# Gate products between the branches' steps, kept in DRAM and read back by the merge: one step of a hybrid decoder on one Trainium2 core

## The chip, the core and the metric

The program runs on one NeuronCore of a Trainium2 chip. The engines are PE (TensorE; PEld is its weight load), DVE (VectorE), ACT (ScalarE), POOL (GpSimd) and SP, whose queue issues most of the DMAs; each executes its own instructions in a fixed order. The metric is the device time of one execution in microseconds (us), the median of several runs. One execution was also taken with the hardware profiler.

## The reference

One layer is computed for a prompt of 1024 tokens and for 8 samples of 8 tokens, with d_model 1024:

```python
n = rmsnorm(x, g_mix);  z = n @ w_in            # gq gk gv gr glr | fq fk fv ff | mq | gt
gates = sigmoid(gt + b_gate).reshape(B, T, 3, 1024)        # gt: 3 * 1024 columns of w_in
o_gla = gla_chunked(...)      # gated linear attention, 4 heads of 128, a state carried over the chunks
o_fox = fox_attend(...)       # softmax attention with forget gates, 8 heads of 64, paged cache for the samples
o_mem = mem_attend(...)       # 4 heads over 256 memory tokens
m = (gates[:, :, 0] * (og @ w_gla_o) + gates[:, :, 1] * (o_fox @ w_fox_o) + gates[:, :, 2] * (o_mem @ w_mem_o))
h = x + m @ w_out
h = h + peer_ffn(rmsnorm(h, g_ffn), ...)   # 8 heads choose 16 of 16384 experts for each token
y = rmsnorm(h, g_final)
```

The expert layer reads one row of two tables (4 KB each) for every token, head and choice. The gates' columns of z depend on the normed input alone; nothing of the branches enters them.

## The kernel before, in words

**Tiling and stages.** The tokens are nine blocks: 0 to 7 of the prompt (128 tokens each) and block 8 with the 64 sample tokens (`SAMPLE`). `base(grp)` computes everything up to the experts' scores for a group of blocks; the groups are [0, 1, 2], [3, 4, 5] and [8, 6, 7], called group 0, 1 and 2 here. NT is the group's number of tokens: 384, 384 and 320. In `base` come: norm and transposes; for each half of the heads the projections, the GLA of each block (`branch1`, then `gla`), the FoX attention (`fox_prompt`); `fox_sample` in group 2; the memory attention; then the merge, the product with w_out, and the scores (w_pq and keys). The part up to the memory attention is called the branch stage below.

**A product.** `mm_w` (L256) loads weights in pieces of 512 KB into one of four `wr` buffers, splits each in two steps into a high part `wh` (ACT, L265) and a low part `wl` (DVE, L267), and multiplies high by high, high by low and low by high. For `proj_T` (L687), which gives a transposed result for 256 columns of w_in, that is 8 x 3 x 2 = 48 matmuls of NT columns (L273, L274, L277), two weight loads, four `wh` and four `wl`. Its results lie in the PSUM banks `pj` (two) and, in group 0, `cw`.

**The merge** (L821 to L842). For each of 3 branches and 4 pieces of 256 columns: one `proj_T` for the gate, the branch's output product (24 matmuls into banks `f`), two sigmoids on ACT from PSUM (L837), and the products and sums on DVE (L839 to L842). So a merge has 12 gate products, 576 matmuls, and 288 matmuls of output products.

**Experts.** Blocks 0, 1, 2, 6 and 7 gather their rows (`peer_gather`): for each, 128 indirect DMAs of 512 KB for u (issued by POOL, L1040; used by DVE, L1042) and 128 for v (L1051; L1057), through four row buffers. Blocks 3, 4, 5 and 8 go through a dense stage at the end (`peer_dense`): both tables are read as a whole, split and multiplied on PE. The weights of that stage (`expert_weights`) are made during group 2. The gathers of blocks 0 to 2 start when group 0 has its scores and run beside groups 1 and 2; those of blocks 6 and 7 start when group 2 has its scores and run beside the dense stage.

**What sets the order.** A scheduler goes through the program by priorities: the code of `base` in the order in which it is written, the choice of experts ahead of it, the gathers far behind. An instruction stands on its engine where the scheduler expects its inputs and a free buffer. The buffers of one name are given out in the order of the program, so a gate product of the merge can only get a `pj` bank when all the projections written before it have had theirs. On the chip each engine then keeps that fixed order.

Of the kernel before, what the change touches and what calls it, by code (L numbers as in the profile page):

```python
# [54 lines left out]
def tile_hybrid(ctx: ExitStack, tc: tile.TileContext, x_prompt, x_sample, cache_fox_k, cache_fox_v,  # L55
# [572 lines left out]
    x2_scr = [dp.tile([128, 1024], F32, name=f"x2_scr{b}") for b in range(9)]  # L628
    o_scr = [dp.tile([128, 3, 4, 128], F32, name=f"o_scr{b}") for b in range(9)]
# [6 lines left out]
    def base(grp):  # L636
# [50 lines left out]
        def proj_T(col):  # L687
            pz, jobs = jobs_T(NT, acT)
            mm_w(wi, 8, col, jobs)
            return pz  # L690

        for half in range(2):
# [45 lines left out]
            branch1(grp[0])  # L738
            kT = T("kv", [128, 2, 1024])
# [37 lines left out]
            for b in grp[1:2]:  # L777
                branch1(b)
            proj(C_FV + half * 256, fin_v)
            for b in grp[2:]:  # L780
                branch1(b)
            pq = proj_T(C_FQ + half * 256)
# [5 lines left out]
            for b in grp:  # L788
                if b != SAMPLE:
                    o = out_tile(b)  # L790
                    fox_prompt(b, half, qT[:, :, off[b]:off[b] + 128], kT, vv, o)
                    put(b, 1, half, o)

        if SAMPLE in grp:
            o = [out_tile(SAMPLE), out_tile(SAMPLE)]
            fox_sample(lfs[0], o)
            for half in range(2):
                put(SAMPLE, 1, half, o[half])
# [21 lines left out]

        m = [T("z", [128, 2, NT]) for _ in range(4)]  # L821
        for br, wo in enumerate((w_gla_o, w_fox_o, w_mem_o)):
# [7 lines left out]
            for c in range(4):  # L830
                pz = proj_T(C_GT + br * 1024 + c * 256)
                po, jobs = jobs_T(NT, (oh, ol), "f")
                mm_w(wo[0], 4, c * 256, jobs)
                for j in range(2):
                    s = T("X", [128, NT])
                    g = br * 8 + c * 2 + j
                    A.activation(s, pz[j], AF.Sigmoid, bias=bgT[:, g:g + 1])  # L837
                    if br == 0:
                        V.tensor_tensor(m[c][:, j], po[j], s, op=OP.mult)  # L839
                    else:  # L840
                        V.tensor_tensor(s, po[j], s, op=OP.mult)
                        V.tensor_tensor(m[c][:, j], m[c][:, j], s, op=OP.add)  # L842
# [397 lines left out]
    def fox_sample(lfn, oT):  # L1240
# [45 lines left out]
        for st in range(4):  # L1286
            pc = [PS("f"), PS("f")]
# [207 lines left out]
```

## Time and profile before

| | |
|---|---|
| device time, median of 3 | 4426.75 us (4417.42 to 4428.59) |
| the profiled execution | 4433.77 us, its span 4432.0 us |
| busy share of the span | PE 85%, PEld 74%, DVE 75%, ACT 41%, POOL 38% |
| HBM traffic | 257 GB/s over the span, 1073 MB read and 64 MB written |
| mean granted TensorE clock | 0.89 |

Busy shares are means over stages that differ; the prediction reads them stage by stage. Matmuls are pipelined: the mean duration of one in the groups is longer than the distance from one to the next, so that the cost of a row of matmuls is read from a stretch of time and the number in it. A wait is put down to the event that came last. Where an engine is idle and is not the one that others wait for, nothing is lost.

### The profile page before, as it was taken

To read this page: it belongs to the slowest core of one execution; us is meant where nothing else is said; L and a number is where in the kernel's file an instruction comes from. 1 tells how busy PE (TensorE), PEld (TensorE's weight loads), DVE (VectorE), ACT (ScalarE), POOL (GpSimd) and SP (SyncE) were. 2 spreads that over 40 slices of the span, in tenths; PEclk is the share of its full clock that TensorE was granted. 3 is DMA by queue.
4 is the path that set the end of the run, shared out by engine and by line. 5 is a ranking of instruction groups with operands and counts; after the bars stand their busy time and mean duration, and the time that the engine had idled before them with its cause. 6 is when DMAs were issued, how large, how long until landed. Compare 5 with 4: busy or idle time off the path is not lost. (4 is left out here: it accounts for less than half of the span.)

```text
span 4432.0 us, 62344 instructions
## 1 busy us (share of the span) xinstructions
PE 3755.6 (85%) x21306; PEld 3288.8 (74%) x21306; DVE 3346.1 (75%) x7924; ACT 1796.2 (41%) x3637; POOL 1679.1 (38%) x1466
## 2 busy tenths in 40 slices
PE   4998998676689775787679979986999999999998
PEld 4886997564378775575556558875999899999997
DVE  3443469988788898888885457578999888888883
ACT  2555444343343333465564334444333223323332
POOL 0000003545644444534455553003445454545530
PEclk8997998787689886677689989997999999999999
DMA  3322457888899987778788899548999999999982
GB/s 110 90 84 70 131 165 227 279 274 294 277 309 332 319 267 242 260 243 273 253 277 287 307 321 320 169 140 289 329 303 339 327 332 337 341 337 327 344 297 81
DMA packets 652340, 1141.32 MB, mean 258 GB/s; under 512 B 62158, under 2 KB 445798, under 8 KB 648439
## 3 DMA queue, kind: packets, MB, share of 16 engines
q0 software_dynamic: 193616, 704.99, 45.6%
q1 hardware_dynamic: 458406, 432.35, 30.3%
q8 instruction: 169, 2.77, 0.2%
q14 instruction: 149, 1.21, 0.1%
HBM read 1073.45 MB, written 63.74 MB: 257 GB/s over the span
## 5 line engine op out<-in xcount | busy, mean ns | idle before, releaser
L1040 POOL DMA_INDIRECT u<-in_peer_u_dram,ei x640 | 783.3, 1224 | 873.2 <-DVE a L1042 347.6
L1051 POOL DMA_INDIRECT v<-in_peer_v_dram,ei x640 | 762.3, 1191 | 865.0 <-DVE acc L1057 452.6
L1042 DVE CUSTOM_DVE_ANT_0 u<-u,x 128x1024 f32<-128x1024 f32 x640 | 774.2, 1219 | 129.9 <-DMA u<-in_peer_u_dram,ei 128.3
L1057 DVE SCALAR_TENSOR_TENSOR acc<-v,a,acc 128x1024 f32<-128x1024 f32 x635 | 811.6, 1278 | 70.6 <-DMA v<-in_peer_v_dram,ei 68.2
L265 ACT ACTIVATE wh<-wr 128x512 fp32r<-128x512 f32 x568 | 354.0, 630 | 595.0 <-PE pj L274 186.2
L267 DVE TENSOR_TENSOR wl<-wr,wh 128x512 fp32r<-128x512 f32 x568 | 386.6, 685 | 219.4 <-PE pj L277 63.8
L1210 PE MATMUL py<-dwh,dvh 128*128 128x448 f32 x1024 | 373.9, 370 | 31.3 <-ACT dwh L1197 28.6
L1187 PE MATMUL pa<-xh,duh 128*128 128x448 f32 x1024 | 384.8, 376 | 1.3 <-ACT duh L1168 1.3
L1188 PE MATMUL pa<-xl,duh 128*128 128x448 f32 x1024 | 379.0, 370 | 0.0
L273 PE MATMUL pj<-aT,wh 128*128 128x384 f32 (+1 forms) x1104 | 367.3, 337 | 11.4 <-ACT X L837 4.5
L1211 PE MATMUL py<-dwl,dvh 128*128 128x448 f32 x1024 | 375.4, 367 | 1.4 <-DVE dwl L1198 1.4
L1212 PE MATMUL py<-dwh,dvl 128*128 128x448 f32 x1024 | 373.4, 368 | 0.3 <-DVE dvl L1206 0.3
L274 PE MATMUL pj<-aT,wh 128*128 128x384 f32 (+1 forms) x1104 | 362.3, 332 | 1.7 <-DVE aT L317 1.7
L281 PE MATMUL pj<-wh,aT 128*128 128x256 f32 x944 | 262.1, 301 | 30.3 <-DVE z L720 10.9
L1205 ACT ACTIVATE dvh<-dvr 128x1024 fp32r<-128x1024 f32 x128 | 134.2, 1059 | 377.2 <-PE py L1211 206.6
L282 PE MATMUL pj<-wh,aT 128*128 128x256 f32 x944 | 258.8, 297 | 2.9 <-DVE aT L847 1.5
L277 PE MATMUL pj<-aT,wl 128*128 128x384 f32 (+1 forms) x1104 | 251.8, 335 | 10.3 <-DVE wl L267 10.1
L1117 PE MATMUL cw<-hot,hot 128*128 128x128 f32 x768 | 173.9, 363 | 92.7 <-ACT stg L1118 73.8
L1190 PE MATMUL pa<-xh,dul 128*128 128x448 f32 x1024 | 240.2, 369 | 0.0
L1117 PEld LDWEIGHTS cw<-hot,hot 128*128 128x128 f32 x768 | 134.8, 248 | 138.1 <-ACT stg L1118 103.3
L1210 PEld LDWEIGHTS py<-dwh,dvh 128*128 128x128 f32 x1024 | 192.4, 189 | 48.6 <-ACT dwh L1197 28.9
L273 PEld LDWEIGHTS pj<-aT,wh 128*128 128x128 f32 x1104 | 213.1, 193 | 17.4 <-ACT X L837 6.6
(475 smaller groups left out, 8439.3 us busy)
## 6 DMA issues: line engine op xcount, KB each, us to landing
wr<-in_w_in_dram SPq DMA_DIRECT2D x168, 512.0 KB, 4.8
dvr<-in_peer_v_dram SPq DMA_DIRECT2D x128, 512.0 KB, 7.5
dur<-in_peer_u_dram SPq DMA_DIRECT2D x128, 512.0 KB, 6.6
dc<-c_scr SPq DMA_DIRECT2D x15, 1792.0 KB, 17.4
wr<-in_w_pq_dram SPq DMA_DIRECT2D x48, 512.0 KB, 4.3
c_scr<-stg SPq DMA_DIRECT2D x24, 1024.0 KB, 6.9
wr<-in_w_out_dram SPq DMA_DIRECT2D x24, 512.0 KB, 4.8
u<-in_peer_u_dram,ei POOLq DMA_INDIRECT x640, 6.2
```

Of the source, the lines that this page charges most:

```text
L267: V.tensor_tensor(wl, raw[:, q2:q2 + 2], wh.bitcast(F32), op=OP.subtract)
L273: PE.matmul(ps, wh[:, i, c], hi[:, k], start=k == 0, stop=False)
L274: PE.matmul(ps, wh[:, i, c], lo[:, k], start=False, stop=False)
L1040: G.indirect_dma_start(out=r, out_offset=None, in_=UR, in_offset=bass.IndirectOffsetOnAxis(ap=ei[:, s:s + 1], axis=0))
L1042: V.tensor_tensor_reduce(r, r, x2, 1.0, 0.0, OP.mult, OP.add, a[:, s:s + 1])
L1051: G.indirect_dma_start(out=r, out_offset=None, in_=VR, in_offset=bass.IndirectOffsetOnAxis(ap=ei[:, s:s + 1], axis=0))
L1057: V.scalar_tensor_tensor(acc, r, a[:, s:s + 1], acc, op0=OP.mult, op1=OP.add)
L1187: PE.matmul(pa[:, :NT], uh[:, k], xh[:, k], start=k == 0, stop=False)
L1188: PE.matmul(pa[:, :NT], uh[:, k], xl[:, k], start=False, stop=False)
L1210: PE.matmul(py[:, :NT], vh[:, j], wh, start=j == 0, stop=False)
L1211: PE.matmul(py[:, :NT], vh[:, j], wl, start=False, stop=False)
L1212: PE.matmul(py[:, :NT], vl[:, j], wh, start=False, stop=j == DG - 1)
```

## The change

The gate products leave the merge. `gate_jobs` is a generator with 12 steps: each computes one gate product, copies the two results from PSUM to a tile `tq` (ACT), and stores it in DRAM (`gate_scr`, 393 KB, in group 2 328 KB). `fill(n)` runs n steps of it. It is called after FoX of each prompt block (one step in the first half, two in the second), after GLA of each block in the second half, before each of the four rounds of `fox_sample`, and with 12 ahead of the merge for what is left. In groups 0 and 1 all 12 steps are used up by then; in group 2 nine are, and three go to `fox_sample`. The merge loads each piece back into a `tq` buffer (two of them), applies the sigmoid in place on ACT, and its output products use `pj` and `f` banks in turn.

```diff
--- before.py
+++ after.py
@@ -626,6 +626,8 @@
     c_scr = dp.tile([sum(64 if b == SAMPLE else 128 for b in DENSE) // 16, 128, 2048], F32, name="c_scr")
     q_scr = dp.tile([128, 4, 64], F32, name="q_scr")
     x2_scr = [dp.tile([128, 1024], F32, name=f"x2_scr{b}") for b in range(9)]
+
+    gate_scr = [dp.tile([12, 128, 2, 384], F32, name=f"gate_scr{i}") for i in range(len(GROUPS))]
     o_scr = [dp.tile([128, 3, 4, 128], F32, name=f"o_scr{b}") for b in range(9)]
 
     def xsrc(b):
@@ -689,6 +691,23 @@
             mm_w(wi, 8, col, jobs)
             return pz
 
+        def gate_jobs():
+
+            for i in range(12):
+                pz = proj_T(C_GT + i * 256)
+                t = T("tq", [128, 2, NT])
+                for j in range(2):
+                    evac(t[:, j], pz[j])
+                SP.dma_start(gscr[i, :, :, :NT], t)
+                yield
+
+        gscr = gate_scr[GROUPS.index(grp)]
+        gates = gate_jobs()
+
+        def fill(n=1):
+            for _ in range(n):
+                next(gates, None)
+
         for half in range(2):
             z = {}
 
@@ -736,6 +755,7 @@
                 put(b, 0, half, o)
 
             branch1(grp[0])
+            fill(half)
             kT = T("kv", [128, 2, 1024])
             vv = T("kv", [128, 8, 256])
             first = min(grp)
@@ -776,9 +796,11 @@
             proj(C_FK + half * 256, fin_k)
             for b in grp[1:2]:
                 branch1(b)
+                fill(half)
             proj(C_FV + half * 256, fin_v)
             for b in grp[2:]:
                 branch1(b)
+                fill(half)
             pq = proj_T(C_FQ + half * 256)
             qT = T("zq", [128, 2, NT])
             for j in range(2):
@@ -790,10 +812,11 @@
                     o = out_tile(b)
                     fox_prompt(b, half, qT[:, :, off[b]:off[b] + 128], kT, vv, o)
                     put(b, 1, half, o)
+                    fill(1 + half)
 
         if SAMPLE in grp:
             o = [out_tile(SAMPLE), out_tile(SAMPLE)]
-            fox_sample(lfs[0], o)
+            fox_sample(lfs[0], o, fill)
             for half in range(2):
                 put(SAMPLE, 1, half, o[half])
         sqm = {}
@@ -818,6 +841,7 @@
                 put(SAMPLE, 2, half, o[half])
 
 
+        fill(12)
         m = [T("z", [128, 2, NT]) for _ in range(4)]
         for br, wo in enumerate((w_gla_o, w_fox_o, w_mem_o)):
             oh, ol = T("kv", [128, 4, NT], F32R), T("kv", [128, 4, NT], F32R)
@@ -828,13 +852,14 @@
                 A.activation(hi, o, AF.Copy)
                 V.tensor_tensor(lo, o, hi.bitcast(F32), op=OP.subtract)
             for c in range(4):
-                pz = proj_T(C_GT + br * 1024 + c * 256)
-                po, jobs = jobs_T(NT, (oh, ol), "f")
+                gt = T("tq", [128, 2, NT])
+                SP.dma_start(gt, gscr[br * 4 + c, :, :, :NT])
+                po, jobs = jobs_T(NT, (oh, ol), "f" if c % 2 else "pj")
                 mm_w(wo[0], 4, c * 256, jobs)
                 for j in range(2):
-                    s = T("X", [128, NT])
+                    s = gt[:, j]
                     g = br * 8 + c * 2 + j
-                    A.activation(s, pz[j], AF.Sigmoid, bias=bgT[:, g:g + 1])
+                    A.activation(s, s, AF.Sigmoid, bias=bgT[:, g:g + 1])
                     if br == 0:
                         V.tensor_tensor(m[c][:, j], po[j], s, op=OP.mult)
                     else:
@@ -1237,7 +1262,7 @@
         G.indirect_dma_start(out=out, out_offset=None, in_=src,
                              in_offset=bass.IndirectOffsetOnAxis(ap=idx, axis=0))
 
-    def fox_sample(lfn, oT):
+    def fox_sample(lfn, oT, fill):
         KR = cache_fox_k[0].rearrange("n (p e) h d -> (n p) (e h d)", e=2)
         VR = cache_fox_v[0].rearrange("n (p e) h d -> (n p) (e h d)", e=2)
 
@@ -1284,6 +1309,7 @@
                              qn[r, j].rearrange("p (b t) -> p b t", t=8), AF.Copy)
         V.tensor_copy(kn, p[:, :256].rearrange("p (j n) -> p j n", n=64))
         for st in range(4):
+            fill()
             pc = [PS("f"), PS("f")]
             pn = PS("po")
             for bb in range(2):
```

How the scheduler places this is seen in the order of the instructions. On PE, at the last GLA of group 1's second half (L438, L446 and L424 are steps of `gla`, with its decay tiles `XL`; L273, L274 and L277 with an output in `pj` are a projection or gate product): before, the steps of GLA follow each other, 122 matmuls of them without anything else between;

```order
L424 MATMUL g_11968<-c_99,lh_11932 128x256
L424 MATMUL g_11968<-c_99,lh_11933 128x256
L438 MATMUL po_11947<-XL_11956 64x64 x2
L438 MATMUL po_11947<-XL_11956 32x32 x4
L438 MATMUL po_11947<-XL_11973 16x16 x8
L446 MATMUL g_11988<-XL_11973 128x128 x2
L424 MATMUL g_11992<-c_99,lh_11932 128x256
```

in the change a piece of a gate product stands ahead of the same steps, and more behind them:

```order
L273 MATMUL pj_13544<-aT_9660,wh_13563 128x384
L274 MATMUL pj_13544<-aT_9661,wh_13563 128x384
L277 MATMUL pj_13544<-aT_9660,wl_13565 128x384
L438 MATMUL po_12294<-XL_12303 64x64 x2
L438 MATMUL po_12294<-XL_12303 32x32 x4
L438 MATMUL po_12294<-XL_12320 16x16 x8
L446 MATMUL g_12335<-XL_12320 128x128 x2
L424 MATMUL g_12339<-c_99,lh_12279 128x256
```

Seven of group 1's twelve gate products stand between steps of GLA in the second half and three in the first; the other two stand among the steps of FoX.

On SP, in the merge of group 1: before, two loads of gate weights stand ahead of each load of a branch's output weights;

```order
L262 DMA wr_13438<-in_w_in_dram 128x4x256
L262 DMA wr_13472<-in_w_in_dram 128x4x256
L262 DMA wr_13508<-in_w_gla_o_dram 128x4x256
L262 DMA wr_13564<-in_w_in_dram 128x4x256
L262 DMA wr_13598<-in_w_in_dram 128x4x256
L262 DMA wr_13634<-in_w_fox_o_dram 128x4x256
```

in the change one load of a kept gate product (`tq`) stands there; the output weights run three pieces ahead of it, through the four `wr` buffers:

```order
L856 DMA tq_14123<-gate_scr_315 128x768
L262 DMA wr_14269<-in_w_fox_o_dram 128x4x256
L1093 DMA gf_7894<-in_g_final_dram 128x1024
L961 DMA ch_1_7982<-t_scr_286 128x256
L856 DMA tq_14165<-gate_scr_315 128x768
L262 DMA wr_14313<-in_w_fox_o_dram 128x4x256
L856 DMA tq_14221<-gate_scr_315 128x768
L262 DMA wr_14357<-in_w_fox_o_dram 128x4x256
```

On DVE the uses of gathered rows (L1042 and L1057) stand between the other work. Counted in its order, 259 of the 768 of blocks 0 to 2 stand ahead of the first product of group 1's merge before and 253 in the change; 324 and 282 ahead of its end; 404 and 362 when group 1's scores are done; 748 and 692 ahead of group 2's merge; 768 and 716 at its end. In both programs all 768 stand ahead of the dense stage.

## The prediction

> **What bounds the kernel now.** I read the page first, then the busy time in stretches cut at the kernel's stages, then the groups and DMAs inside the stretches that the change touches. The page's head:
>
> ```profile
> span 4432.0 us, 62344 instructions
> ```
>
> The stretches (columns: stretch and its length; busy time and number of instructions on PE, PEld, DVE, ACT, POOL; granted clock, DMA share, GB/s) are, in order: group 0's branch stage and its merge; group 1's branch stage, merge, and w_out with scores; group 2's branch stage, merge, and w_out with scores; the dense stage.
>
> ```profile
> 100.00:425.00 325.00, 291.80 (x1942) 252.18 (x1942) 123.99 (x339) 176.60 (x397) 5.71 (x13) 0.89 0.26 76
> 425.00:580.00 155.00, 154.08 (x897) 153.04 (x897) 75.15 (x124) 66.32 (x114) 0.00 (x0) 0.98 0.47 139
> ...
> 705.00:1285.00 580.00, 405.34 (x2292) 329.68 (x2290) 492.71 (x1267) 236.52 (x502) 309.12 (x273) 0.76 0.85 284
> 1285.00:1455.00 170.00, 152.64 (x825) 145.31 (x826) 155.72 (x325) 69.50 (x113) 84.05 (x70) 0.96 0.94 330
> 1455.00:1685.00 230.00, 178.51 (x1114) 167.76 (x1114) 209.09 (x643) 77.91 (x165) 92.91 (x86) 0.87 0.87 284
> 1685.00:2690.00 1005.00, 772.65 (x4254) 570.59 (x4254) 735.76 (x1879) 498.44 (x1145) 507.99 (x433) 0.79 0.81 277
> 2690.00:2815.00 125.00, 121.86 (x812) 121.30 (x813) 91.03 (x137) 57.46 (x103) 23.32 (x20) 0.97 0.76 250
> 2815.00:2950.00 135.00, 115.24 (x806) 110.12 (x805) 82.49 (x356) 53.82 (x123) 3.83 (x9) 0.93 0.47 150
> ...
> 3090.00:4410.00 1320.00, 1311.75 (x6866) 1204.42 (x6864) 1116.81 (x1810) 405.53 (x643) 597.38 (x484) 1.00 0.90 311
> ```
>
> The dense stage is PE from end to end (1312 of 1320 us) at the full clock, and it needs group 2's results. So the time is: when group 2 is done, plus a stage that the change leaves alone. The merges are PE too (154 of 155, 153 of 170, 122 of 125 us). The branch stages of groups 1 and 2 aren't: PE is busy 405 of 580 and 773 of 1005 us, at a clock of 0.76 and 0.79, beside a DVE at 85% and 73%.
>
> What PE waits for there is seen in GLA of group 1's second half. First the stretch (and one of the first half), then its waits (group of instructions | busy, mean ns | idle before <- releaser):
>
> ```profile
> 1050.00:1150.00 100.00, 44.06 (x235) 35.84 (x233) 83.04 (x160) 24.00 (x47) 58.45 (x56) 0.56 0.85 283
> 850.00:900.00 50.00, 19.80 (x93) 15.58 (x94) 46.02 (x154) 12.61 (x24) 29.03 (x26) 0.53 0.78 251
> 1300.00:1450.00 150.00, 138.48 (x767) 131.86 (x766) 136.94 (x256) 62.90 (x102) 74.76 (x63) 1.00 0.94 329
> ```
>
> ```profile
> L446 PE MATMUL g<-XL 128*128 128x128 f32 x48 | 12.2, 418 | 17.3 <-DVE XL L434 17.1
> ```
>
> PE idles 56 of 100 us, its matmuls of 418 ns waiting for a DVE that works on gathered rows between the steps of the chain. Here PE has room, and the merge has none.
>
> **The change, part by part.** *Price of a gate product on PE.* Busy time over number in the three merges is 154.08/897 = 0.172, 152.64/825 = 0.185 and 121.86/812 = 0.150 us for a matmul, so 48 of them are 8.3, 8.9 and 7.2 us, and 12 products 99, 107 and 86: 292 us leave the merges and come back in the branch stages. The other engines' price:
>
> ```profile
> L267 DVE TENSOR_TENSOR wl<-wr,wh 128x512 fp32r<-128x512 f32 x568 | 386.6, 685 | 219.4 <-PE pj L277 63.8 <-PE pj L285 39.4 <-issue 27.5
> L265 ACT ACTIVATE wh<-wr 128x512 fp32r<-128x512 f32 x568 | 354.0, 630 | 595.0 <-PE pj L274 186.2 <-PE pj L282 161.2 <-DVE wl L267 58.7
> L837 ACT ACTIVATE X<-pj,c 128x384 f32<-128x384 f32 (+1 forms) x64 | 33.3, 552 | 16.3 <-PE pj L277 16.1
> L842 DVE TENSOR_TENSOR z<-z,X 128x384 f32<-128x384 f32 (+1 forms) x48 | 24.4, 527 | 0.0
> ```
>
> A product moves four `wl`, 2.7 us of DVE, so 33 us a group, and four `wh` on ACT. New are two copies out of PSUM; the nearest row is the sigmoid at 552 ns, so a group's ACT gets 12 x (2.5 + 1.1) = 43 us more in its branch stage. ACT is busy there 177 of 325, 237 of 580 and 498 of 1005 us: hidden. SP gets 24 DMAs a group and 12 x (393 or 328 KB) each way, 27 MB in all.
>
> *The merges.* 288 matmuls stay: 50, 53 and 43 us of PE. The new chain is the read back through two `tq` buffers: a piece is loaded, gets two sigmoids (1.1 us) and up to four DVE operations (2.1 us), and only then frees its buffer for the next load but one. Loads of nearly its size in the same three stretches (KB each, us to landing):
>
> ```profile
> P<-o_scr SPq DMA_DIRECT2D x9, 256.0 KB, 4.1
> ...
> wr<-in_w_in_dram SPq DMA_DIRECT2D x19, 512.0 KB, 6.6
> ...
> P<-o_scr SPq DMA_DIRECT2D x5, 256.0 KB, 6.5
> ```
>
> So a piece takes (4.1 + 3.2)/2 = 3.7, (6.6 + 3.2)/2 = 4.9 and 4.9 us, and 12 of them 44, 59 and 58. In groups 1 and 2 DVE may come last instead, by the gathers under it. Their issues on POOL (u, then v) in group 1's branch stage and merge, in group 2's branch stage, and behind it, and the price of using one:
>
> ```profile
> 705.00:1285.00 580.00, 154.33 (x131) 0.76 0.85 284
> 1285.00:1455.00 170.00, 54.37 (x46) 0.96 0.94 330
> 1685.00:2690.00 1005.00, 217.80 (x176) 0.79 0.81 277
> ...
> 705.00:1285.00 580.00, 146.69 (x128) 0.76 0.85 284
> 1285.00:1455.00 170.00, 29.10 (x23) 0.96 0.94 330
> 1685.00:2690.00 1005.00, 205.00 (x174) 0.79 0.81 277
> 2690.00:2950.00 260.00, 20.57 (x18) 0.95 0.61 198
> ...
> L1042 DVE CUSTOM_DVE_ANT_0 u<-u,x 128x1024 f32<-128x1024 f32 x640 | 774.2, 1219 | 129.9 <-DMA u<-in_peer_u_dram,ei 128.3
> L1057 DVE SCALAR_TENSOR_TENSOR acc<-v,a,acc 128x1024 f32<-128x1024 f32 x635 | 811.6, 1278 | 70.6 <-DMA v<-in_peer_v_dram,ei 68.2
> ```
>
> Group 1's merge had 69 gathers; by DVE's order it now has 29. DVE then needs 156 - 33 - 40 x 1.25 = 73 us. Group 2's goes from 18 to 24: 91 - 33 + 8 = 66. I take the later of the chains, and 56 us for group 0 (its 50 of PE and one load and cast to start): the merges become 56, 73 and 66 us and give 99 + 97 + 59 = 255.
>
> *Group 0's branch stage.* PE idles 325 - 292 = 33 us there, so of 99 us at least 66 show at the present clock; full cost is 99. Were the 292 us at a clock of 1.00 and not 0.89, 32 us more would fit, so 34 is the other end. I take 60, near the idle time's 66: there is no gather here to keep the clock low.
>
> *Group 1's.* By pace: 259 gathers took 580 us, 2.24 us each; DVE's order has 253 ahead of the merge now, 567 us, so 13 less. By DVE's load: 33 us more of `wl` and six gathers (8 us) less, on an engine at 85%: 25 more. I take the middle, 6 more.
>
> *Group 2's.* By pace: 350 took 1005 us, 2.87 each, and 14 fewer stand there (330 instead of 344 in the order): 40 less. By load: 33 - 14 x 1.25, 15 more. The middle: 12 less.
>
> *Behind group 2's merge* 52 gathers are left, where 18 were issued from the merge on before, and the dense stage stands behind all of them on DVE: 82 + 52 x 1.25 = 147 us of DVE in a stretch of 135, so 12 more; 0 if half of them are out by then.
>
> The sum: 255 - 60 - 6 + 12 - 12 = 189 us. From the profiled execution's 4434 us (span 4432.0) that leaves 4245. The median of the runs is 4427, 7 us below that execution, so I predict **4238 us**.
>
> *The clock, against the change.* The three stretches above show 0.53 and 0.56 where the gate products go, and 1.00 where they come from. [...] I keep 189: the middle values above are not PE's.
>
> **The rivals.**
>
> *A. The low clock stays.* The ten products of group 1 that stand between steps of GLA run at 0.56: 8.9/0.56 = 15.9, 7 us more each; nine in group 2's branch stage at its mean of 0.79, 1.9 us more each; and PE's fixed order hands that on to the chain: 87 us. For it: the rows of 0.53 and 0.56. Against: the products themselves fill the gaps. 4245 + 87 - 7 = 4325; with merges held up by slow read backs up to 4400.
>
> *B. The gathers become the bound.* The dense stage stands behind 768 gathers on DVE. In the profile the last are issued 18 x 2.9 = 52 us past 2690; group 0 ends 39 us earlier, so the gathers are used by 2703 at the same pace, where group 2 ended at 2950. The gain can't pass 247 us: 4180. For it: DMA at 0.81 to 0.94 and 27 MB more of it. Against: it takes all of the branch stages' price at its lower ends.
>
> *C. Slower: PE's order makes the chain wait.* GLA's steps now stand behind pieces of products that need weights through SP, ACT and DVE; whatever those miss, the chain, its gathers on DVE and the FoX behind it miss too. The merges give 255 and the tail takes 12, so at 243/36 = 6.8 us of delay for a product nothing is won; at the full 8.1 us (292/36) it is 49 us slower, 4476, and any wait for weights comes on top. For it: DMA at 0.85 and weights landing in 6.6 us under the gathers. Against: 56 idle us in 100, and in group 0, where little is idle, a product is priced at 5 us.
>
> *D. Nothing.* Delays of about 6.8 us a product, within 13 us of before.
>
> That the products stay in the merge isn't among them: PE's order has them between the branches' steps.
>
> **How the numbers follow.** The forecast's own range comes from its bounds: 20 us either way on the merges, group 0 at 34 or 99, the others at their ends. The lower end is cut at the gathers' bound: 4180; the upper is 255 - 20 - 99 - 25 - 15 - 12 = 84 us of gain: 4343. Chances: forecast 0.52, A 0.20, B 0.12, D 0.05, C 0.11. The range for 8 in 10 goes from 4165 (a little past B) to 4405 (all of A); D and C lie above it. About 0.3%, 13 us, is what a measurement of this kernel can tell from no change. Faster by more: forecast, A and B, 0.84; same: D, 0.05; slower: C, 0.11.
>
> **What would show each step.** The merges: stretches of 56, 73 and 66 us between the first and last sigmoid of a group, instead of 155, 170 and 125. Hidden products: PE in GLA of group 1's second half busy well over 44%, at a clock over 0.56, with the stretch not longer than now. Group 0: its branch stage 60 us longer. The dense stage: 1320 us as now, some 190 us earlier. The prediction is wrong if GLA's waits go from DVE `XL` to `wl` or to weights in front of it, if the merges' waits go to `tq`'s loads at more than 5 us a piece, or if the dense stage begins right behind the last gather of block 2, which is B.

## The result and the profile after

The changed kernel took 4322.52 us (median of 4 runs, 4307.64 to 4330.27), beside 4427.28 for the kernel before: a ratio of 0.9769, 95% interval 0.9743 to 0.9795. Run once more, in another series, it took 4338.05 us, ratio 0.9812 (0.9779 to 0.9844). So it is faster, by some 100 us; 4238 us and 189 us of gain were forecast. The measured time lies in the range, and little more than half of the forecast gain is there.

The stretches of the two profiles (columns as in the prediction: stretch and its length; busy time and number on PE, PEld, DVE, ACT, POOL; granted clock, DMA share, GB/s) are cut here at one event in both: a branch stage ends with PE's last matmul of the memory attention, and the merge behind it ends when its result has been split for the product with w_out (to within some us). In the changed kernel, in order: group 0's branch stage and merge; group 1's branch stage, merge, and w_out with scores; the same three of group 2; the dense stage.

```profile
span 4324.1 us, 62414 instructions
```

```profile
100.00:485.00 385.00, 368.90 (x2526) 335.77 (x2525) 156.41 (x388) 221.16 (x479) 6.77 (x13) 0.98 0.38 114
485.00:549.00 64.00, 58.55 (x341) 57.08 (x340) 42.89 (x75) 34.56 (x58) 0.00 (x0) 0.95 0.60 193
...
680.00:1282.00 602.00, 485.97 (x2797) 412.24 (x2796) 505.70 (x1262) 268.79 (x566) 312.27 (x266) 0.83 0.87 293
1282.00:1386.00 104.00, 75.00 (x360) 68.90 (x360) 98.95 (x239) 41.87 (x68) 44.71 (x39) 0.84 0.94 334
...
1386.00:1591.00 205.00, 159.58 (x948) 148.97 (x949) 187.36 (x593) 68.33 (x149) 95.06 (x81) 0.86 0.87 289
...
1591.00:2600.00 1009.00, 831.14 (x4893) 637.26 (x4891) 749.67 (x1924) 532.33 (x1223) 501.18 (x416) 0.85 0.83 285
2600.00:2690.00 90.00, 62.03 (x360) 58.16 (x360) 82.18 (x139) 39.31 (x68) 41.96 (x33) 0.85 0.97 340
...
2690.00:2846.00 156.00, 117.43 (x760) 107.71 (x761) 137.39 (x404) 57.64 (x127) 55.60 (x57) 0.85 0.91 307
...
2846.00:4324.00 1478.00, 1401.31 (x7325) 1280.66 (x7323) 1234.67 (x2288) 474.16 (x797) 619.75 (x524) 0.98 0.87 301
```

The branch stages and merges of the kernel before, by the same cuts:

```profile
100.00:436.00 336.00, 302.30 (x1994) 262.27 (x1994) 127.27 (x344) 182.73 (x409) 5.71 (x13) 0.88 0.27 79
436.00:581.00 145.00, 144.58 (x854) 143.94 (x853) 72.46 (x119) 60.28 (x102) 0.00 (x0) 1.00 0.47 138
711.00:1284.00 573.00, 401.43 (x2278) 326.76 (x2276) 486.32 (x1225) 233.49 (x497) 308.54 (x271) 0.76 0.85 284
1284.00:1464.00 180.00, 160.41 (x883) 152.54 (x881) 164.40 (x335) 73.04 (x120) 87.54 (x74) 0.96 0.94 333
1669.00:2678.00 1009.00, 775.72 (x4284) 574.22 (x4284) 743.01 (x1922) 499.08 (x1146) 507.91 (x434) 0.79 0.81 276
2678.00:2824.00 146.00, 138.81 (x938) 137.50 (x937) 106.97 (x163) 67.08 (x119) 28.22 (x24) 0.98 0.78 259
```

The other cuts of before lie at 1669 us (group 1's scores are done) and 2963 us (the dense stage begins). The prediction cut its stretches up to 16 us beside these, so that a length there can differ by as much. Beside each other in us, with the second profile of the changed kernel:

| stretch | before | change | change again | forecast difference | measured |
|---|---|---|---|---|---|
| group 0's branch stage (from 100 us) | 336 | 385 | 397 | +60 | +49, +61 |
| its merge | 145 | 64 | 64 | -99 | **-81, -81** |
| its w_out and scores | 130 | 131 | 131 | 0 | +1 |
| group 1's branch stage | 573 | 602 | 599 | +6 | **+29, +26** |
| its merge | 180 | 104 | 103 | -97 | **-76, -77** |
| w_out, scores | 205 | 205 | 207 | 0 | 0, +2 |
| group 2's branch stage | 1009 | 1009 | 1012 | -12 | 0, +3 |
| its merge | 146 | 90 | 90 | -59 | -56 |
| behind it, to the dense stage | 139 | 156 | 158 | +12 | +17, +19 |
| dense stage to the end | 1469 | 1478 | 1469 | 0 | +9, 0 |

The merges won 213 and 214 us of the 255 that were forecast; the branch stages took 78 and 90 where 54 were. So some half of the 81 to 87 us that are missing are the merges of groups 0 and 1, and the largest part of the rest is group 1's branch stage, 20 to 23 us beside its forecast.

What a product meets in GLA of group 1's second half, in the changed kernel: the stretch, then PE's groups in it (group of instructions | busy, mean ns | idle before <- releaser).

```profile
1072.00:1160.00 88.00, 67.80 (x399) 60.11 (x398) 70.77 (x136) 43.11 (x80) 43.21 (x39) 0.82 0.87 298
```

The same stretch before, and the chain's own matmuls in it:

```profile
1072.00:1157.00 85.00, 36.80 (x175) 27.86 (x174) 70.39 (x132) 23.58 (x45) 50.13 (x50) 0.52 0.84 276
...
L446 PE MATMUL g<-XL 128*128 128x128 f32 x32 | 8.9, 446 | 12.3 <-DVE XL L434 12.1
```

PE's groups in the change:

```profile
L273 PE MATMUL pj<-aT,wh 128*128 128x384 f32 x72 | 24.3, 340 | 0.7 <-ACT tq L99 0.7
...
L446 PE MATMUL g<-XL 128*128 128x128 f32 x32 | 6.6, 357 | 4.8 <-DVE XL L434 4.6
```

PE is busy 77% where it was 43%, the granted clock is 0.82 where it was 0.52, and the chain's own matmuls (L446) went from 446 to 357 ns. With the products in the gaps the clock is higher there.

### The profile page after: what moved, and what is told of

Read it like the earlier page. It is cut to its first block, busy times and chain, and to the rows that moved or that the text cites. A ratio compares the mean times of both kernels' runs of the same rounds, so it can differ in the third digit from the quotient of the medians.

```text
span 4324.1 us, 62414 instructions
## 1 busy us (share of the span) xinstructions
PE 3719.4 (86%) x21306; PEld 3260.5 (75%) x21306; DVE 3338.8 (77%) x7924; ACT 1821.1 (42%) x3710; POOL 1691.6 (39%) x1466
## 5 line engine op out<-in xcount | busy, mean ns | idle before, releaser
L273 PE MATMUL pj<-aT,wh 128*128 128x384 f32 (+1 forms) x1104 | 373.6, 344 | 12.1 <-ACT tq L99 7.3
L274 PE MATMUL pj<-aT,wh 128*128 128x384 f32 (+1 forms) x1104 | 367.9, 337 | 1.5 <-DVE aT L317 1.5
L277 PE MATMUL pj<-aT,wl 128*128 128x384 f32 (+1 forms) x1104 | 261.6, 341 | 5.8 <-DVE wl L267 5.8
L273 PEld LDWEIGHTS pj<-aT,wh 128*128 128x128 f32 x1104 | 217.2, 197 | 19.2 <-ACT tq L99 11.4
L281 PEld LDWEIGHTS pj<-wh,aT 128*128 128x128 f32 x944 | 193.4, 206 | 43.0 <-DVE z L739 8.2
L274 PEld LDWEIGHTS pj<-aT,wh 128*128 128x128 f32 x1104 | 217.6, 197 | 2.8 <-DVE aT L317 2.4
```

The source lines that it names most:

```text
L273: PE.matmul(ps, wh[:, i, c], hi[:, k], start=k == 0, stop=False)
L274: PE.matmul(ps, wh[:, i, c], lo[:, k], start=False, stop=False)
L281: PE.matmul(ps, hi[:, k, :], wh[:, i], start=k == 0 and first, stop=False)
```

## The experiments

Four explanations of what group 1's and group 2's branch stages pay were put to the test: **DVE** (the products' splits load the engine on which the gathers stand), **PE** (it has less room than its mean says), **traffic** (weights and spill slow the gathers), and **order** (the scheduler puts another number of gathered rows ahead of the merges). All kernels are edits of the changed one (the diffs below show their main lines), and each ratio is to runs of the kernel before in the same series. In the table, group 1's branch stage ends with the last matmul of the memory attention, and "rows" is the number of gathered rows that DVE used in it; a group "to w_out" is counted from the end of the scores ahead of it; the stretch runs from group 0's scores to the dense stage. Stage lengths, rows and busy times are those of the profiled execution. The expectations count the branch stages of groups 1 and 2 up to one of the merge's sigmoids, 15 and 23 us later, in the changed kernel: their 617 and 1032 us are 602 and 1009 here. Their 574 us of before ends with the memory attention, so what they call 43 us more is 29, and their 8 us more in group 2 are none.

| kernel | ratio to before, 95% | group 1's branch: us (rows; PE, DVE busy) | group 1 to w_out | group 2 to w_out | stretch | dense |
|---|---|---|---|---|---|---|
| before | 1 | 573 (255; 401, 486) | 753 | 1155 | 2252 | 1469 |
| change | 0.9769 (0.9743 to 0.9795) | 602 (249; 486, 506) | 706 | 1099 | 2166 | 1478 |
| change again | 0.9812 (0.9779 to 0.9844) | 599 (250; 488, 508) | 702 | 1102 | 2169 | 1469 |
| no splits | 0.9704 (0.9674 to 0.9735) | 587 (242; 480, 468) | 692 | 1104 | 2160 | 1470 |
| no round trip | 0.9874 (0.9847 to 0.9901) | 604 (255; 484, 513) | 715 | 1136 | 2207 | 1482 |
| all at the merge | 1.0090 (1.0063 to 1.0117) | 586 (256; 421, 495) | 772 | 1170 | 2277 | 1463 |
| behind GLA only | 0.9865 (0.9821 to 0.9910) | 612 (251; 489, 508) | 717 | 1147 | 2219 | 1472 |
| a quarter of the weights | 0.9780 (0.9743 to 0.9817) | 613 (260; 486, 522) | 702 | 1133 | 2182 | 1462 |
| a third of the matmuls | 0.9659 (0.9613 to 0.9705) | 570 (228; 426, 479) | 659 | 1118 | 2155 | 1470 |
| behind FoX only | 0.9855 (0.9817 to 0.9893) | 591 (246; 483, 501) | 698 | 1131 | 2185 | 1468 |
| one pass | 0.9502 (0.9470 to 0.9535) | 549 (214; 425, 435) | 637 | 1100 | 2118 | 1469 |
| no gate products | 0.9483 (0.9447 to 0.9518) | 566 (252; 403, 479) | 673 | 1091 | 2113 | 1471 |
| five row buffers | 0.9876 (0.9838 to 0.9913) | 617 (270; 490, 540) | 707 | 1184 | 2248 | 1461 |
| three row buffers | 0.9888 (0.9852 to 0.9923) | 596 (218; 480, 470) | 682 | 1091 | 2146 | 1556 |

**No splits.**

```diff
-                wl = T("wl", [128, 2, 256], F32R)
-                V.tensor_tensor(wl, raw[:, q2:q2 + 2], wh.bitcast(F32), op=OP.subtract)
+                wl = wh            # in the gate products alone
```

> Left out: the low part of the gate weights. In the 36 gate products `wh` stands in the place of `wl`, so PE has the same 48 matmuls for a product, and DVE loses 4 x 36 splits of 685 ns, 33 us a group; the gates come out less exact. The changed kernel took 4322 us; its branch stages, from group 1's on, are 617 us (43 more than before, where 6 were predicted) and 1032 us (8 more, where -12 was predicted). Theory DVE (the branch stages of groups 1 and 2 pay for the splits, since DVE is at 84% there and its gathers stand behind them): group 1's branch stage falls by 25 to 40 us to 577 to 592, group 2's by 15 to 33, the time to 4250 to 4285. Theory PE (they pay because PE has no room in the FoX stretches): nothing of PE's work is gone, group 1's branch stage stays within 10 us of 617, and the time is 4300 to 4325. Theory DMA (they pay for the spill's traffic): as PE.

(The high part is then counted twice, so the gates' inputs come out nearly doubled, not just less exact; the work is as stated.) The time was 4302.0 us, at the lower end of PE's theory. DVE fell by 38 to 40 us in group 1's branch stage (7 to 8 rows fewer were used in it), the stage by 12 to 15, group 1 to w_out by 10 to 14, and group 2 not at all.

```profile
676.00:1263.00 587.00, 479.55 (x2797) 408.58 (x2797) 467.52 (x1207) 270.65 (x565) 307.78 (x260) 0.84 0.87 294
```

DVE was idle 20% of the stage now. The stage won less than half of what DVE did, so DVE's splits are at most a part of what it pays for.

**No round trip.**

```diff
-                SP.dma_start(gscr[i, :, :, :NT], t)
+                kept[0] = t
-                gt = T("tq", [128, 2, NT])
-                SP.dma_start(gt, gscr[br * 4 + c, :, :, :NT])
-                    A.activation(s, s, AF.Sigmoid, bias=bgT[:, g:g + 1])
+                    A.activation(s, kept[0][:, j], AF.Sigmoid, bias=bgT[:, g:g + 1])
```

> Left out: the store of the 12 pieces and their read back. Each gate product is still computed and copied to `tq`, but every piece of the merge takes the last one of the group (so 11 of 12 gates are wrong), with the sigmoid written to an `X` buffer as in the kernel before. 4.7 MB of stores leave each branch stage and 4.7 MB of loads each merge. Theory DMA (the spill delays the gathers, which set the pace of the branch stage): at the stage's 295 GB/s 4.7 MB are 16 us, so group 1's branch stage falls from 617 to about 601 and group 2's 1032 by as much; group 0's merge falls from 73 to 56 us, as its loads of 5.3 us go; time 4265 to 4285. Theories DVE and PE: the branch stages stay within 6 us; only group 0's merge falls, and the merges of groups 1 and 2 (89 and 67 us), where DVE was busy 86 and 63 us, do not; time 4295 to 4315.

It took 4375.12 us, which no theory had. The spill itself costs group 1's branch stage nothing: 604 us with 255 rows, as with it (602 and 599). The loss lies elsewhere. In group 2 the scheduler now put more rows ahead of the merge (723 used before it by the trace, 693 in the change), and group 2 took 37 us more; and in group 0 the granted clock was 0.72 in the stretch of the last section (0.97 in the change), and that stretch and the merge behind it took 137 us and not 124. The spill was cheap where it stands, as the DMA's own rows of the changed kernel show (KB each, median us to landing):

```profile
gate_scr<-tq SPq DMA_DIRECT2D x24, 384.0 KB, 5.2
tq<-gate_scr SPq DMA_DIRECT2D x24, 384.0 KB, 4.4
...
tq<-gate_scr SPq DMA_DIRECT2D x12, 320.0 KB, 7.6
```

**All at the merge.**

```diff
-                next(gates, None)
+                next(gates, None) if n == 12 else None
```

> Only the placement is undone: all 12 gate products of a group are computed just ahead of the merge, and still stored and read back. Theory (all of the gain is work in gaps of PE): the branch stages go back to those of the kernel before (325, 574 and 1024 us within 10), the stretch from the memory attention to the last sigmoid grows to that of before and a little more by the read back at the end (155 to 175, 179 to 200, 131 to 145), and the time is 4420 to 4470, not faster than before. Rival (a good part comes from the merge's new form: its output products no longer share their bank with nothing else to do, since the gate is ready): the time stays under 4395.

4467.96 us, slower than before by 0.9%: the theory's range. So the gain is the placement; without it, the spill and the new form of the merge cost some 35 us. (Group 1's branch stage, 586 us, is 13 longer than before; 10 were expected at most.)

**Behind GLA only**, and **behind FoX only.**

```diff
-            fill(half)             # behind branch1, three places
+            fill(2)
-                    fill(1 + half) # behind fox_prompt
```

> The same 12 products, all behind GLA of a block (two behind each, in both halves), none behind FoX or in `fox_sample`. In the changed kernel FoX of group 1's first half took 140 us with PE busy 137 at a clock of 1.00 (129 with 106 before), and GLA of its second half 88 with 68 (85 with 37 before). Theory PE (a product is free in GLA's gaps and costs its full price in FoX): FoX falls back to 129 to 132, the first GLA stretches grow by 1 us a product, 6 in all, group 1's branch stage is 605 to 612, and the time 4295 to 4315. Theory DVE (a product costs its splits wherever it stands): group 1's branch stage stays at 617 within 6 and the time at 4310 to 4330. Rival (the gaps of GLA hold no more than they have, the chain waits for products): GLA of the first half grows by over 15 us and the time is over 4335.

```diff
-            fill(half)             # behind branch1, three places
-                    fill(1 + half) # behind fox_prompt
+                    fill(2)
```

> The same 12 products, none behind GLA: two behind FoX of each prompt block, and in group 2 the last four in the rounds of `fox_sample`. In group 2 the dense stage's weights are made in the gaps of GLA: 486 of their matmuls stood ahead of the end of GLA before, 430 with the change and 438 with all products behind GLA, and the stretch from there to the merge grew from 477 to 501 and 525 us. Theory displaced work (gate products push those weights out of GLA's gaps): ahead of the end of GLA stand 470 or more again and group 2's branch stage, 1032 us, falls by 10 to 25; group 1, which makes no such weights, loses the free gaps of its second GLA and is 5 to 20 us longer; time 4300 to 4330. Rival (GLA's gaps are the cheap place for both groups): both groups' branch stages grow, by 15 us or more each; time over 4345.

4371.45 and 4353.11 us. Neither place is better than the mixture (behind FoX, 0.9855, is not clear of the change in the same series, 0.9812), and the stage-by-stage expectations failed in both. Behind GLA, FoX of group 1's first half did not fall back but took 141 us, with 549 matmuls of products and projections in it (530 in the change): products written behind a block's GLA still run under what follows it. Behind FoX, group 1's branch stage was 8 to 11 us shorter where 5 to 20 more was expected, and group 2's 23 to 26 us longer where 10 to 25 less was; 458 matmuls for the dense stage's weights stood ahead of the end of GLA, not 470. That products displace those weights was seen (486, 430 and 438 in the three kernels of the expectation), but that this is what group 2 pays for was not shown. Group 2 to w_out varies from 1099 to 1147 us over kernels with the same products between the steps and four row buffers, for reasons that stay open.

**A quarter of the weights.**

```diff
+            elif q == 0:           # gate products: one piece, used for all
+                SP.dma_start(raw[:, :2], src[:256, col:col + 256].rearrange("(k p) n -> p k n", p=128))
-                A.activation(wh, raw[:, q2:q2 + 2], AF.Copy)
+                part = raw[:, :2] if gate else raw[:, q2:q2 + 2]
+                A.activation(wh, part, AF.Copy)
```

> Left out: three quarters of the gate weights' loads. A gate product loads one piece of 256 KB and uses it for all of its 48 matmuls and splits, instead of two pieces of 512 KB; PE, ACT and DVE do as much as before, on other numbers. That takes 9.4 MB of DMA from each group. Group 1's branch stage used 255 gathered rows before and with the change; it took 574 us then and 617 now, 2.25 and 2.42 us a row. Theory traffic (the weights that moved in with the products slow the gathers): at 295 GB/s 9.4 MB are 32 us, so the pace falls to 2.25 to 2.32 us a row there, group 2's branch stage falls by as much, and the time to 4240 to 4275. Theory PE (products in PE's fixed order delay the chain, and the gathers behind it on DVE): the pace stays at 2.38 to 2.45 and the time at 4305 to 4330.

4330.0 us, as the change: traffic falls. 9.4 MB less for each group bought no time. The pace in group 1's branch stage, by the expectation's cut 631/265 = 2.38 us a row, is where PE's theory begins, not at 2.25 to 2.32; up to the end of the memory attention it is 613/260 = 2.36, beside 2.42 and 2.40 in the change and 2.25 before. Group 1 reached w_out as soon as in the change (702 us), group 2 31 to 34 us later.

**A third of the matmuls.**

```diff
-                            PE.matmul(ps, wh[:, i, c], lo[:, k], start=False, stop=False)
+                            if not gate:
+                                PE.matmul(ps, wh[:, i, c], lo[:, k], start=False, stop=False)
-                        for i in range(2):
+                        for i in range(0 if gate else 2):
```

> Left out: two thirds of the gate products' matmuls (high by low and low by high; the gates come out less exact). Loads, splits, copies and the round trip stay. At 499.76/2863 us a matmul 12 x 32 of them are 67 us of PE in group 1's branch stage. Theory PE: the pace of that stage falls from 2.42 to 2.25 to 2.32 us a gathered row, the stage to 574 to 592 us, group 2's by 10 to 30, and group 0's branch stage from 375 to about 342; time 4210 to 4270. Theory traffic: groups 1 and 2 keep their pace (2.38 or more), only group 0 gains its 33 us; time 4280 to 4300.

4266.44 us, the PE theory's time. Group 1's branch stage fell by 29 to 32 us to 570 (587 by the expectation's cut, as PE's theory has it); its pace did not fall (570/228 = 2.50), because 21 rows fewer stood in it, and group 2 did not gain (1118 us to w_out, against 1099 and 1102). Group 0 gained 36 to 48 us of the total.

```profile
644.00:1214.00 570.00, 425.72 (x2416) 349.69 (x2414) 479.01 (x1242) 264.63 (x564) 287.04 (x246) 0.80 0.87 290
```

**The change again.**

> The changed kernel once more, for the spread of a stage from one profile to the next. All theories: time 4322 within 15, every stage within 8 us of its first value.

4338.05 us, 16 us above the first median; group 1's and 2's stages within 4 us of the first profile. Two stretches lie outside the expectation: group 0's w_out came 12 us later, beside a granted clock of 0.69 in the stretch of the last section, where the first profile has 0.97, and the dense stage was 9 us shorter.

**One pass**, and **no gate products.** The first is the third of the matmuls and no split; the second:

```diff
-                pz = proj_T(C_GT + i * 256)
-                t = T("tq", [128, 2, NT])
-                for j in range(2):
-                    evac(t[:, j], pz[j])
-                SP.dma_start(gscr[i, :, :, :NT], t)
                 yield
-                SP.dma_start(gt, gscr[br * 4 + c, :, :, :NT])
+                G.memset(gt, 0.0)
```

> Left out: of each gate product the matmuls high by low and low by high, and the splits for them (less exact gates). PE and DVE are relieved together, 67 and 33 us in a group, where they were relieved one at a time so far. The stretch from group 0's scores to the dense stage took 2252 us before, 2166 and 2169 with the change, 2160 without the splits, 2155 with a third of the matmuls. Theory two limits (either engine alone is enough to hold the branch stages): the stretch falls below 2120 us, group 0 gains its 45 us, and the time is 4190 to 4235. Theory gathers (the 768 rows of blocks 0 to 2, which end 20 us ahead of the dense stage with the change, 200 us ahead before, now set the stretch, whatever PE and DVE do for the products): the stretch stays at 2135 to 2165 and the time at 4245 to 4280.

> Left out: the gate products altogether, with their loads, splits, copies and the round trip; the merge takes the sigmoid of a tile of zeros and the bias. What is left is the changed kernel with products at no price. Theory price (the products cost the branch stages what they grew by, 41 us in group 1, some 10 in group 2, 50 in group 0): the stretch from group 0's scores to the dense stage falls from 2166 by 50 us or more to 2115 or less, and the time is 4190 to 4225. Theory gathers: the stretch stays within 35 us of 2166, at 2130 or more, since the rows still have to be gathered; only group 0's 50 us are won, and the time is 4240 to 4280.

4220.76 and 4211.28 us: the theory of two limits, and the theory of a price, had these times. The last kernel is the measure for the rest: it has the change's merge and nearly as many rows in group 1's branch stage (252, beside 249 and 250), and what is gone is the products, with their loads, splits, copies and round trip. Here are its group 1's branch stage, FoX of the first half (with the second half's projections and first GLA, which stand among it), and GLA of the second; then FoX of the kernel before, of the change, and of the kernels without splits, with products behind FoX only, and with three row buffers; last, of those with a third of the matmuls and with one pass.

```profile
627.00:1193.00 566.00, 402.60 (x2223) 323.37 (x2221) 478.72 (x1215) 225.59 (x488) 315.42 (x270) 0.74 0.85 282
...
872.00:1000.00 128.00, 108.15 (x651) 85.68 (x650) 99.83 (x187) 61.41 (x138) 66.01 (x57) 0.90 0.87 288
1000.00:1078.00 78.00, 36.06 (x173) 27.55 (x172) 64.81 (x124) 23.03 (x44) 49.00 (x45) 0.50 0.83 276
```

```profile
943.00:1072.00 129.00, 106.40 (x648) 83.92 (x646) 104.13 (x211) 64.01 (x139) 66.13 (x58) 0.91 0.86 291
```

```profile
932.00:1072.00 140.00, 137.46 (x872) 116.84 (x871) 110.41 (x205) 76.94 (x169) 68.97 (x57) 1.00 0.90 302
```

```profile
919.00:1057.00 138.00, 135.84 (x843) 115.92 (x843) 94.06 (x175) 77.06 (x166) 61.37 (x54) 0.96 0.88 300
```

```profile
950.00:1081.00 131.00, 122.25 (x757) 101.21 (x756) 104.89 (x193) 71.11 (x152) 64.81 (x58) 0.95 0.89 302
```

```profile
934.00:1077.00 143.00, 135.59 (x852) 115.01 (x851) 104.07 (x191) 75.87 (x167) 57.16 (x54) 0.99 0.86 283
```

```profile
896.00:1030.00 134.00, 121.14 (x724) 98.47 (x723) 106.28 (x203) 80.59 (x178) 53.53 (x50) 0.93 0.90 307
```

```profile
877.00:998.00 121.00, 112.61 (x712) 91.01 (x712) 81.83 (x159) 82.65 (x180) 51.66 (x45) 0.99 0.90 308
```

Where FoX has 843 to 872 matmuls it takes 138 to 143 us, with PE busy 95 to 98% of it at a clock of 0.96 to 1.00, and DVE busy 94 or 110 us makes no difference. So in the change this stretch is PE's. Below that the number of matmuls does not set the length alone: 648 and 651 take 129 and 128 us and 757 take 131, but 724 take 134, and 712 take 121, with DVE busy 82 us where it is 100 to 106 in the other four. GLA of the second half looked free (88 us after 85), but against the kernel without products it is not: 88 us for 33 rows, 78 us for 39.

Over the whole of group 1's branch stage, the kernels with four or three row buffers and all of the products' PE work in it (480 to 489 us busy) take 587 to 613 us, with DVE busy 468 to 522 us and 218 to 260 rows used; those without the products there (before and no products, 401 and 403 us) take 573 and 566. So the change put 83 to 87 us of PE into the stage, and they cost 26 to 36 of its time, 0.3 to 0.4 us each. That both reliefs together win back more than their sum (of the stretch's 2166 us, 6 without splits, 11 with a third of the matmuls, 48 with one pass) agrees with two limits, but 40 rows had also moved from the stretch into the dense stage, so this run doesn't separate the second limit from the order.

**Five and three row buffers.**

```diff
-ROWS, ROWS2 = 4, 5
+ROWS, ROWS2 = 5, 5                # and WR = 3; the other kernel: ROWS, ROWS2 = 3, 5
```

> The changed kernel with five row buffers for the gathers of blocks 0 to 2 instead of four, and three weight buffers `wr` instead of four. The scheduler then puts more rows ahead of the merges on DVE (421 instead of 380 and 1149 instead of 1045 of its instructions for gathered rows). Theory gathers (their pace sets the stretch to the dense stage): the 768 rows, 2139 us from first to last use, go through at least 80 us sooner, and the time falls below 4300. Rival (DVE's order: each row that stands ahead of the merge delays the chain of the branches by the 1.6 us or so that a row cost from kernel to kernel): group 2 ends later, the dense stage begins over 100 us behind the last row again, and the time is over 4345.

> The changed kernel with three row buffers instead of four up to the dense stage (five in it, as now). The scheduler then leaves more rows to the dense stage: 938 of DVE's instructions for gathered rows stand ahead of group 2's product with w_out, 1085 now. Where the products were computed in one pass, 40 rows more went into the dense stage, and it took 1469 us all the same. Theory order (what a stage lasts follows from the rows that stand ahead in DVE's order; from kernel to kernel group 1 cost some 1.7 us for each row, and rows in the dense stage are free as long as DVE has time there): the stretch from group 0's scores to the dense stage falls from 2166 to 2000 to 2070, the dense stage grows to 1500 to 1540 as DVE fills up, and the time is 4215 to 4290, below the 4322 and 4338 of now. Rival (a row needs its buffer for the time of its load, and with three of them DVE waits): DVE's waits for rows grow by over 100 us, the pace in group 1's branch stage goes from 2.42 us a row to over 2.8, the stretch stays over 2150, and the time is over 4350.

4390.53 and 4384.88 us: the rivals' times. With five, all rows of blocks 0 to 2 were used ahead of group 2's w_out, and group 2 took 82 to 85 us more. With three, 90 rows went into the dense stage and the stretch lost only 20 us. The rival's reasons did not quite come: DVE's waits for rows grew by 95 us (124 to 219) where over 100 were expected, the stretch was 2146 us and not over 2150. Group 1's branch stage took 596 us, 3 to 6 less, with 31 to 32 rows less in it, so what a stage lasts does not simply follow from the rows in it; since DVE also waited longer, this does not rule the order out. The time was lost where no theory had it, in the dense stage, which filled up to 1556 us.

```profile
692.00:1288.00 596.00, 480.37 (x2797) 405.08 (x2796) 469.56 (x1221) 264.64 (x561) 244.81 (x234) 0.84 0.82 268
...
2838.00:4394.00 1556.00, 1420.43 (x7323) 1291.53 (x7322) 1344.24 (x2422) 474.12 (x801) 751.06 (x614) 0.95 0.91 317
```

In the one-pass kernel the same stage took 40 rows more at no price:

```profile
2757.00:4226.00 1469.00, 1406.66 (x7327) 1286.54 (x7327) 1284.87 (x2347) 477.76 (x801) 661.01 (x562) 0.98 0.91 317
```

No version that computes the whole of the gate products beat the change. The four that are faster (no splits, a third of the matmuls, one pass, no products) each leave out a part of every product or all of it.

## Why the prediction was right, and where it was off

**What bounds the kernel**: right. Merges and the dense stage were PE's (busy 145 of 145, 160 of 180 and 139 of 146 us, and 1312 of 1320 by the prediction's cut), and taking the products out of the merges gave 81, 76 and 56 us (99, 97 and 59 forecast). The forecast of a gain is borne out by its mechanism; its size was off, in three terms above all, and the range of 4165 to 4405 us was wide enough to hold that.

**Group 0's merge**: mis-sized, 81 us for 99. Without any product group 0 reached w_out at 498 us where it had been 581: at most 83 us were to be had. The trace shows why: from the end of the memory attention on, PE's matmuls fall from 854 to 341, by 513 and not by 576, since the merge's first gate products had run beside the memory attention before. And PE, which had no idle time in this stretch, now idles 5 to 6 us of 64.

**Group 1's merge**: mis-sized, 76 and 77 us for 97. It ended on DVE, as forecast, but DVE is busy 99 of 104 us, where 73 were forecast: by this cut it used 37 gathered rows there and not 29 (10 us), and the sum had started from 156 us in a stretch that ended 9 us short of w_out (164 up to there).

**Group 0's branch stage**: right. 60 us were forecast; against before it took 49 and 61 us more, against the kernel without products 50 and 62.

**Group 1's branch stage, the step that failed.** The prediction had one reading by pace (13 us less) and one by DVE's load (25 more), took the middle, 6, and set PE's own price aside ("the middle values above are not PE's"). The stage took 29 and 26 us more than before, and 36 and 33 more than without the products. The pace reading failed in its premise: 249 and 250 rows were used and not 255, as its order said, but the pace went from 573/255 = 2.25 to 2.42 and 2.40 us a row. The load reading had the size, but its cause is only a part of it: taking the splits away gave 12 to 15 us. What the middle left out is PE. Taking two thirds of the matmuls away gave 29 to 32 us, though with 21 rows fewer in the stage. A part of PE's price can be followed in FoX of the first half, whose lack of room the mean of the stage hid: PE was idle 129 - 106 = 23 us there (in the trace before), and the order put 872 - 648 = 224 matmuls more there, 31 us of busy time. The excess, 8 us, is most of the 11 us by which this stretch grew. The rest doesn't follow from such a sum. Ahead of FoX (711 to 943 us before, 680 to 932 in the change) PE had been idle 76 of 232 us and got 31 us of work, and the stretch grew by 20 us all the same, 7 more than without the products (245 us). What holds the time there, PE's fixed order, DVE or both, is open.

**Group 2's branch stage**: 12 us less were forecast by the same middle; it took 0 to 3 more, and 17 to 20 more than without products (992 us). Which engine takes them there is open.

**Behind group 2's merge**: 17 and 19 us for 12. The rows came with it, as forecast: 48 in that stretch, none before, and DVE is busy 137 of 156 us where it was busy 86 of 139.

**The rivals.** *A, the low clock*, names 4325 us, within 3 us of the measured median, by a mechanism that is not there, so this is chance: products between GLA's steps run at 336 to 340 ns, as over the whole kernel before (337), at a granted clock of 0.82. *B, the gathers as the bound*, has its sign in the trace. PE's longest wait at the start of the dense stage, in the second profile of the change, is for the end of block 2 (in the first, a wait of 16.4 us in this place is put down to the choice of experts, `ch`):

```profile
PE pt L1175 <- DVE acc L1047: 16.3, 1, 16.3
```

But it is no bound: with one pass the dense stage began 133 us ahead of that end (2757, 2890) and lasted as long. *C and D* did not come: a product costs its branch stage some 3 us in group 1 and 4 to 5 in group 0, below the 6.8 at which the gain is gone.

**The sum.** From before to no products at all are 4433.8 - 4213.1 = 221 us (profiled executions). The change wins about half of that, 102 to 108; the forecast of 189 supposed 85%.

## What to carry to other kernels

Price work that moves into another stage segment by segment: idle time of the engine in each segment, against the work that the order puts just there. A mean of 70% busy hid a segment with 23 us of room that got 31. That sum is a lower bound only: another segment had 76 us of room for the 31 that it got, and grew by 20. Before choosing between two readings, build the bound as well: the kernel without the moved work says what all of the hiding could bring (here 221 us). And cut the two profiles at one and the same instruction, or a stage and its neighbour trade time on paper.

## What the runs showed of the hardware

In one stretch of some 50 us of group 0 (FoX of the second half and the memory attention, in every kernel beside some matmuls of projections) the granted clock is either 0.97 to 1.00 or 0.64 to 0.73: high in 4 profiles and low in 10, and one of each in two executions of the same kernel. Here is the second profile of the change, beside 0.97 in the first:

```profile
423.00:478.00 55.00, 50.11 (x202) 33.44 (x201) 11.42 (x32) 31.44 (x87) 0.00 (x0) 0.69 0.17 55
```

The stretch and the merge behind it take 138 us and not 124. What decides between the two clocks no run shows. The difference is 0.3% of the time that no edit accounts for, the size of several differences above; a stage-by-stage comparison shows it where a median doesn't.
